# Expert weights fetched as 2 KB and 8 KB runs, two blocks to a transfer, with the rows of the expert inputs permuted to match

## The chip, the cores and the metric

The kernel runs on one core of a Trainium2 chip. The metric is device time in microseconds (us); lower is better. All inputs and outputs lie in device memory (HBM) in float32. The engines are called PE (TensorE, matrix products), DVE (VectorE), ACT (ScalarE), POOL (GpSimd) and SP (SyncE, which here only issues transfers).

## The reference

One decoder layer over 512 tokens of width 1024. First a layer norm with modulation from a condition vector, three kinds of attention, an output projection, a residual and a layer norm. Then, on the result `x`, the part that the change is about:

```
h   = LN(x) * (1 + scale2) + shift2
y   = MoE(h)                       # 16 experts in 4 groups; each token: one group, two experts in it
x   = LayerNorm(alpha * x + (1 + gate2) * y)

MoE:  g = h @ w_gate[e]   u = h @ w_up[e]        # [1024 -> 256] each, 16 experts
      a = silu(g) * u * combine[e]
      y = sum over e of a @ w_down[e]            # [256 -> 1024]
```

The weights of the 16 experts are 16 x (2 x 1024 x 256 + 256 x 1024) x 4 bytes = 50.3 MB, the largest input.

## The kernel before, in words

Everything is one function `build`. A scheduler orders the instructions of each engine from the program and a table of numbers `PRM`; the queues are in order, so an instruction that waits holds back all behind it on its engine. SP issues nearly all loads.

Attention and the output projection come first. `outproj(n)` (line 1184) works on 128 tokens: product, layer norm to `x1`, and at line 1238 ACT writes the normalised row block `t2`, which POOL stores to the scratch tensors `xsA_d` (tokens 0 to 255) or `xs_d` in HBM (line 1240). `route(n)` (line 1059) then picks the experts: long chains of small DVE steps, with the products `rkp` (line 1097), `tabp` (1129) and `tabq` (1163) on PE, ending in a table of token numbers (`tokA` at line 1135 after block 1, `tokB` at 1131 after block 3). While PE waits there it runs dummy products called `warm` (line 350).

The expert stage goes over four quarters q of four experts each. `prep(q)` (line 1297) gathers token rows from `xsA_d` and `xs_d` by those tables (POOL, line 1289, three row tiles b of 128 slots), transposes them 128 channels at a time (`gTp`, line 997) and lets ACT apply scale and shift while it copies them to `gT` (line 1002). The scale and the shift of channel block k are columns of `mc2` and `mc1`, one channel to a partition, made by `mod_cols` (line 335). In block k, partition p holds channel 128 k + p.

Per quarter PE then does (lines 1313 to 1321) for each of eight channel blocks k and three row tiles b one set of four products, one per expert, which run side by side on 32 columns each. `gu` collects gate and up together, 512 wide. After silu, product and transposes (`atp`, line 1346; `aT`), lines 1360 to 1372 do the down projection `dn` in two column halves hf of 512, for three b and two blocks f of 128 hidden channels, again four experts side by side. `cmb` and `cmh` (lines 1410, 1418) add up the results per token, DVE and ACT do the last layer norm, and POOL scatters rows to the output (line 1394).

The weights come through a ring of eight buffers of 8 KB per partition (`ewt`, line 1281; six in pool `wst`, two in `wst2`, `PRM["NW"]`). For gate and up, a buffer holds one block k of four experts and is filled by two transfers of 512 KB, in runs of 1 KB (line 1316). For down, a buffer holds one f and one hf of four experts, one transfer of 1 MB in runs of 2 KB (line 1365); so a quarter takes 8 + 4 buffers, and the two down buffers of hf=0 are given back halfway through the down projection. A buffer is refilled when its last product is done.

Of the kernel before, what the change touches and what calls it, by code (L numbers as in the profile page):

```python
# [10 lines left out]
F32 = mybir.dt.float32  # L11
F32R = mybir.dt.float32r
I32 = mybir.dt.int32
AF = mybir.ActivationFunctionType
OP = mybir.AluOpType
# [28 lines left out]
T, D, NT, KD = 512, 1024, 4, 8  # L44
# [64 lines left out]
def build(tc, A, out, dbg=None):  # L109
# [30 lines left out]
    with top:  # L140
# [7 lines left out]
        def wt(name, p):  # L148
            return p.tile([128, 2048], F32, name=name, tag="w")
# [10 lines left out]
        gt_d = dram.tile([4, 512], F32, name="gt_d")  # L160

# [515 lines left out]
        gate_out(0, m1)  # L677
        zc = {"k": kp.tile([128, 16, 32], F32, name="zck"), "v": kp.tile([128, 16, 32], F32, name="zcv")}
# [334 lines left out]
        sc2 = lambda k: mc2[:, k // 4, k % 4:k % 4 + 1]  # L1013
        sh2 = lambda k: mc1[:, 2 + k // 4, k % 4:k % 4 + 1]
# [169 lines left out]
        def outproj(n):  # L1184
# [53 lines left out]
            S.activation(t2, x1, AF.Identity, bias=nm, scale=rs2)  # L1238
# [42 lines left out]
        def ewt(name):  # L1281
            i = cnt_w[0]
            cnt_w[0] += 1
            return wt(name, wst if i % (NW1 + NW2) < NW1 else wst2).rearrange("p (e c) -> p e c", e=4)
# [25 lines left out]
        for q in range(NQ):  # L1310
            gT = gTn
            gu = [psp.tile([128, 512], F32, name=f"gu{b}", tag=("q", "z", "z")[b], bufs=(1, 2, 2)[b]) for b in range(CAPB)]
            for k in range(KD):
                w = ewt(f"gu{q}_{k}")
                for u, nm in enumerate(("moe_w_gate", "moe_w_up")):
                    SP.dma_start(w[:, :, 256 * u:256 * u + 256],
                                 A[nm][4 * q:4 * q + 4, k * 128:(k + 1) * 128].rearrange("e p f -> p e f"))
                for b in range(CAPB):
                    together([lambda e=e: PE.matmul(gu[b][32 * e:32 * e + 32], gT[b][:, k, 32 * e:32 * e + 32], w[:, e],  # L1319
                                                    start=(k == 0), stop=(k == KD - 1), skip_group_check=True)  # L1320
                              for e in range(4)])
# [18 lines left out]
            for b in range(CAPB):  # L1340
                a = ep.tile([128, 256], F32, name="act", bufs=2)
                S.activation(a, gu[b][:, 0:256], AF.Silu)  # L1342
                V.tensor_tensor(a, a, gu[b][:, 256:512], op=OP.mult)  # L1343
                ps = bank("t", "atp2")
                for f in range(2):
                    PE.transpose(ps[:, f * 128:(f + 1) * 128], a[:, f * 128:(f + 1) * 128], ident)
                t = ep.tile([128, 2, 128], F32, name="aT", bufs=4)
                cp(pick("aTe", "V", b), t, heads(ps[:, 0:256], 2))
                aT.append(t)
                s = q * CAPB + b  # L1350
                o = ep.tile([128, GW], F32R, name="oht", bufs=CAPB)
                V.tensor_scalar(o[:, 0:min(GW, 256)], C("pos", 0, min(GW, 256)), tab[:, 2 * NSLOT + s:2 * NSLOT + s + 1], None, op0=OP.is_equal)
                if GP > 128:
                    G.tensor_copy(o[:, 256:320], o[:, 128:192])
                oht.append(o)
# [4 lines left out]
            for hf in range(2):  # L1360
                cs = slice(512 * hf, 512 * hf + 512)
                dn = [psp.tile([128, 512], F32, name=f"dn{b}", tag=("s", "s", "o")[b], bufs=(2, 2, 1)[b]) for b in range(CAPB)]
                wd = [ewt(f"dn{q}_{hf}{f}") for f in range(2)]
                for f in range(2):
                    SP.dma_start(wd[f], A["moe_w_down"][4 * q:4 * q + 4, f * 128:(f + 1) * 128, cs].rearrange("e p c -> p e c"))
                k_ = "3" if q == NQ - 1 else ""

                for b in range(CAPB):
                    for f in range(2):
                        together([lambda b=b, e=e, f=f: PE.matmul(  # L1370
                            dn[b][32 * e:32 * e + 32], aT[b][:, f, 32 * e:32 * e + 32], wd[f][:, e],
# [99 lines left out]
        with tc.If(cnt > CAP), tc.tile_pool(name="bp", bufs=1) as bp:  # L1471
# [19 lines left out]
            with tc.For_i(0, NE, 1) as e:  # L1491
                wg = bp.tile([128, KD, 512], F32, name="bwg")
                wd = bp.tile([128, 2, D], F32, name="bwd")
                for u, nm in enumerate(("moe_w_gate", "moe_w_up")):
                    SP.dma_start(wg[:, :, 256 * u:256 * u + 256],
                                 A[nm][ds(e, 1)].rearrange("a (k p) f -> p (a k) f", p=128))
# [74 lines left out]
```

## Time and profile before

| | us |
|---|---|
| three runs | 591.91, 593.4, 599.62 (median 593.4) |
| the profiled execution | 596.7 |
| its span | 594.8 |
| PE busy in it | 548.7 (92%) |
| DVE busy | 368.2 (62%) |
| ACT busy | 222.1 (37%) |
| POOL busy | 97.4 (16%) |
| mean share of the 16 DMA engines used by SP's loads | 52.9% |
| bytes read from HBM | 112.12 MB |

The span is divided into 40 slices in the page's rows; one slice is 14.9 us. Busy shares are means over stages that have different limits, so what a change is worth has to be read in the stage where it lies. The expert stage is roughly the last third, from 402 us on. A number behind "PEclk" is the clock granted to PE, 1.00 being the higher of its two levels.

### The profile page before, as it was taken

To read this page: it belongs to the slowest core of one execution; us is meant where nothing else is said; L and a number is where in the kernel's file an instruction comes from. 1 tells how busy PE (TensorE), PEld (TensorE's weight loads), DVE (VectorE), ACT (ScalarE), POOL (GpSimd) and SP (SyncE) were. 2 spreads that over 40 slices of the span, in tenths; PEclk is the share of its full clock that TensorE was granted. 3 is DMA by queue.
4 is the path that set the end of the run, shared out by engine and by line. 5 is a ranking of instruction groups with operands and counts; after the bars stand their busy time and mean duration, and the time that the engine had idled before them with its cause. 6 is when DMAs were issued, how large, how long until landed. Compare 5 with 4: busy or idle time off the path is not lost.

```text
span 594.8 us, 10444 instructions
## 1 busy us (share of the span) xinstructions
PE 548.7 (92%) x3856; PEld 333.1 (56%) x3856; DVE 368.2 (62%) x1219; ACT 222.1 (37%) x556; POOL 97.4 (16%) x114
## 2 busy tenths in 40 slices
PE   2899999999899999999899999978899999999990
PEld 1559775687788998755455456653434234234240
DVE  7515656664678568877769568886138157167174
ACT  2514443561428336374634512121434062070130
POOL 0114200000010010003301112123502122011022
PEclk9969999999799999999999999978999999999996
DMA  8993246743930200098300685359699999999601
GB/s 301 373 328 108 83 142 225 260 153 102 323 91 19 72 37 1 2 220 226 124 2 0 222 278 200 119 209 306 164 370 351 366 365 348 374 356 354 248 1 47
DMA packets 77546, 117.05 MB, mean 197 GB/s; under 512 B 7937, under 2 KB 54440, under 8 KB 77492
## 3 DMA queue, kind: packets, MB, share of 16 engines
q1 hardware_dynamic: 72328, 102.60, 52.9%
q0 software_dynamic: 4960, 13.64, 6.3%
q8 instruction: 32, 0.52, 0.4%
q14 instruction: 22, 0.18, 0.1%
q10 hardware_dynamic: 204, 0.11, 0.1%
HBM read 112.12 MB, written 8.40 MB: 203 GB/s over the span
## 4 chain that ended last, share of the span: by engine, by line
PE 78%; DVE 11%; issue 3%; DMA 3%; ACT 2%; POOL 2%; ACTq 0%; POOLq 0%
PE gu L1319 13%; PE zps L407 13%; PE dn L1370 7%; PE onsa L894 6%; PE yps L1215 5%; PE zall L423 3%; PE modps L323 2%; PE modps L375 2%; PE gTp L997 2%; PE cmb L1410 2%; PE stp L501 2%; PE sps L921 2%; PE wps L849 1%; PE warm L356 1%; PE cmh L1418 1%
## 5 line engine op out<-in xcount | busy, mean ns | idle before, releaser
L1319 PE MATMUL gu<-gu,gT 128*32 128x512 f32 x768 | 85.3, 596 | 0.1
L1319 PEld LDWEIGHTS gu<-gu,gT 128*32 128x32 f32 x768 | 23.8, 110 | 52.5 <-issue 50.6
L1370 PE MATMUL dn<-dn,aT 128*32 128x512 f32 x384 | 45.3, 597 | 0.4 <-ACT aT L127 0.2
L1343 DVE TENSOR_TENSOR act<-act,gu 128x256 f32<-128x256 f32 x12 | 5.1, 421 | 59.8 <-ACT act L1342 59.8
L1002 ACT ACTIVATE gT<-gTp,modc,modc 128x128 f32<-128x128 f32 x96 | 35.7, 461 | 10.1 <-PE gTp L997 9.5
L1342 ACT ACTIVATE act<-gu 128x256 f32<-128x256 f32 x12 | 4.6, 387 | 72.1 <-PE gu L1319 72.1
L1215 PE MATMUL yps<-wol,oM 128*128 128x512 f32 x64 | 30.9, 595 | 0.0
L1375 DVE SCALAR_TENSOR_TENSOR y<-dn,tab,gt 128x512 f32<-128x512 f32 x24 | 18.0, 748 | 10.2 <-PE dn L1370 10.2
L323 PE MATMUL modps<-ada,cond 128*32 128x512 f32 x128 | 18.3, 631 | 4.4 <-DVE gr L1079 4.1
L1370 PEld LDWEIGHTS dn<-dn,aT 128*32 128x32 f32 x384 | 10.4, 109 | 20.8 <-issue 18.5
L894 PE MATMUL onsa<-pt,vs 128*64 128x512 f32 x40 | 20.6, 614 | 0.0
L491 ACT ACTIVATE Sg<-Sg,nms 128x128 f32<-128x128 f32 (+3 forms) x32 | 17.8, 559 | 3.7 <-DVE nms L490 3.3
L491 ACT ACTIVATE W<-W,nmw 128x256 f32<-128x256 f32 (+1 forms) x32 | 15.3, 478 | 9.7 <-DVE nmw L490 9.3
L997 PEld LDWEIGHTS gTp<-cf,rows 128*128 128x128 f32 x96 | 10.4, 142 | 15.1 <-ACT gT L1002 9.2
L448 DVE TENSOR_TENSOR rp<-zps,trig 128x128 f32<-128x128 f32 (+1 forms) x28 | 9.7, 345 | 12.9 <-PE zps L407 12.5
L356 PE MATMUL warm<-cf 128*128 128x128 f32 x88 | 17.2, 326 | 0.1
L407 PE MATMUL zps<-B1s,hH 128*128 128x256 f32 x64 | 15.1, 329 | 2.2 <-DVE B1s L210 1.1
L356 PEld LDWEIGHTS warm<-cf 128*128 128x128 f32 x88 | 13.8, 222 | 5.5 <-issue 4.7
L1378 DVE TENSOR_TENSOR ys<-y,ys 128x512 fp32r<-128x512 f32 x22 | 15.2, 692 | 2.1 <-ACT ys L127 1.4
L997 PE MATMUL gTp<-cf,rows 128*128 128x128 f32 x96 | 14.8, 282 | 1.6 <-DMA rows<-xs_d,tokB 1.6
L127 ACT COPY pt<-stp 128x512 f32<-128x512 f32 x14 | 7.9, 586 | 22.2 <-PE stp L501 21.9
L1389 ACT ACTIVATE R<-R,rsf 128x1024 f32<-128x1024 f32 x3 | 3.7, 1241 | 31.4 <-DVE rsf L1388 31.4
(529 smaller groups left out, 1472.7 us busy)
## 6 DMA issues: line engine op xcount, KB each, us to landing
ada<-in_ada_w_dram SPq DMA_DIRECT2D x48, 512.0 KB, 5.9
gu<-in_moe_w_gate_dram SPq DMA_DIRECT2D x32, 512.0 KB, 9.7
gu<-in_moe_w_up_dram SPq DMA_DIRECT2D x32, 512.0 KB, 9.6
dn<-in_moe_w_down_dram SPq DMA_DIRECT2D x16, 1024.0 KB, 10.5
x<-in_x_dram SPq DMA_DIRECT2D x4, 512.0 KB, 4.9
phik<-in_nsa_phi_k_dram SPq DMA_DIRECT2D x4, 512.0 KB, 5.0
phiv<-in_nsa_phi_v_dram SPq DMA_DIRECT2D x4, 512.0 KB, 4.8
wo<-in_w_out_dram SPq DMA_DIRECT2D x8, 256.0 KB, 9.3
```

The lines of the kernel that those rows point to most:

```text
L323: return lambda: PE.matmul(ps[32 * j:32 * j + 32], cond[:, k], t[:, 512 * (j % 2):512 * (j % 2) + 512], start=first, stop=last, skip_group ...
L356: PE.matmul(ps[:, :128], ident, ident, start=True, stop=True)
L407: PE.matmul(ps[:, :w], l[:, k, ts_], get(k, r), start=(k == 0 and i == 0), stop=(k == KD - 1 and i == 2))
L423: m = PE.matmul(outs[n], l[:, k, n * 128:(n + 1) * 128], get(k, r), start=(beg and n % 2 == 0), stop=(k == KD - 1 and i == 2), skip_group_ ...
L491: S.activation(S_h, S_h, AF.Exp, bias=nm, scale=-1.0, accum_out=den)
L894: PE.matmul(ops[64 * g:64 * g + 64, cols], lhsT, rhs, start=first[g], stop=False, skip_group_check=True)
L997: PE.transpose(ps[:, k * 128:(k + 1) * 128], src[:, (4 * a + k) * 128:(4 * a + k + 1) * 128], ident)
L1002: S.activation(dst[:, kk], pk, AF.Identity, bias=sh2(kk), scale=sc2(kk))
L1215: last = PE.matmul(ps, l, r[:, cs], start=(i == 0), stop=(i == len(order) - 1))
L1319: together([lambda e=e: PE.matmul(gu[b][32 * e:32 * e + 32], gT[b][:, k, 32 * e:32 * e + 32], w[:, e], start=(k == 0), stop=(k == KD - 1), ...
L1370: together([lambda b=b, e=e, f=f: PE.matmul(dn[b][32 * e:32 * e + 32], aT[b][:, f, 32 * e:32 * e + 32], wd[f][:, e], start=(f == 0), stop= ...
L1375: V.scalar_tensor_tensor(y, dn[b], tab[:, s:s + 1], gt2[:, cs], op0=OP.mult, op1=OP.mult)
```

## The change

The gate and up weights of two neighbouring blocks come in one buffer. Partition p now holds channels 8 p to 8 p + 7 instead of p, 128 + p, 256 + p and so on, so that two blocks k, k + 1 lie next to each other in HBM: runs of 2 KB at a pitch of 8 KB, four experts, 1 MB per transfer. The down weights of two experts come in one buffer with hidden channels 2 p and 2 p + 1 on partition p: runs of 8 KB, 2 MB per transfer, both halves hf and both f in it. The ring has four buffers of 16 KB instead of eight of 8 KB. To match, `t2` is written with its channels permuted, the transposes of the activations read every second column, and scale and shift of the gathered rows come from a new tile `mpk`, which is made by a trip through HBM (`md_d`: two small stores, two small loads).

```diff
-    "NW": [6, 2, 3, 5], ...
+    "NW": [3, 1, 3, 5], ...
         def wt(name, p):
-            return p.tile([128, 2048], F32, name=name, tag="w")
+            return p.tile([128, 4096], F32, name=name, tag="w")
+        md_d = dram.tile([4, 512], F32, name="md_d")
         gate_out(0, m1)
+        SP.dma_start(md_d[0:2], m1[64:128:32])
...
-        sc2 = lambda k: mc2[:, k // 4, k % 4:k % 4 + 1]
-        sh2 = lambda k: mc1[:, 2 + k // 4, k % 4:k % 4 + 1]
+        SP.dma_start(md_d[2:4], m2[0:64:32])
+        mpk = cst.tile([128, 2, KD], F32, name="mpk")
+        for a in range(2):
+            SP.dma_start(mpk[:, a], md_d[2 * a:2 * a + 2].rearrange("a (p k) -> (a p) k", k=KD))
+        V.tensor_scalar(mpk[:, 1], mpk[:, 1], 1.0, None, op0=OP.add)
+        sc2 = lambda k: mpk[:, 1, k:k + 1]
+        sh2 = lambda k: mpk[:, 0, k:k + 1]
...
-            S.activation(t2, x1, AF.Identity, bias=nm, scale=rs2)
+            S.activation(t2.rearrange("t (k p) -> t p k", k=KD), x1.rearrange("t (p k) -> t p k", k=KD), AF.Identity,
+                             bias=nm, scale=rs2)
...
             for k in range(KD):
-                w = ewt(f"gu{q}_{k}")
-                for u, nm in enumerate(("moe_w_gate", "moe_w_up")):
-                    SP.dma_start(w[:, :, 256 * u:256 * u + 256],
-                                 A[nm][4 * q:4 * q + 4, k * 128:(k + 1) * 128].rearrange("e p f -> p e f"))
+                if k % 2 == 0:
+                    wg = ewt(f"gu{q}_{k}").rearrange("p (e u k f) -> p e u k f", e=4, u=2, k=2)
+                    for u, nm in enumerate(("moe_w_gate", "moe_w_up")):
+                        SP.dma_start(wg[:, :, u], A[nm][4 * q:4 * q + 4].rearrange("e (p k) f -> p e k f", k=KD)[:, :, k:k + 2])
                 for b in range(CAPB):
-                    ... gT[b][:, k, 32 * e:32 * e + 32], w[:, e],
+                    ... gT[b][:, k, 32 * e:32 * e + 32], wg[:, e, :, k % 2],
...
-                    PE.transpose(ps[:, f * 128:(f + 1) * 128], a[:, f * 128:(f + 1) * 128], ident)
+                    PE.transpose(ps[:, f * 128:(f + 1) * 128], a[:, f:256:2], ident)
...
-                wd = [ewt(f"dn{q}_{hf}{f}") for f in range(2)]
-                for f in range(2):
-                    SP.dma_start(wd[f], A["moe_w_down"][4 * q:4 * q + 4, f * 128:(f + 1) * 128, cs].rearrange("e p c -> p e c"))
+                if hf == 0:
+                    wd = [ewt(f"dn{q}_{a}").rearrange("p (e f c) -> p e f c", e=2, f=2) for a in range(2)]
+                    for a in range(2):
+                        SP.dma_start(wd[a], A["moe_w_down"][4 * q + 2 * a:4 * q + 2 * a + 2].rearrange("e (p f) c -> p e f c", f=2))
...
-                            ... aT[b][:, f, 32 * e:32 * e + 32], wd[f][:, e],
+                            ... aT[b][:, f, 32 * e:32 * e + 32], wd[e // 2][:, e % 2, f, cs],
```

The branch for overfull experts behind the stage is changed in the same way; it is not entered with these inputs.

The change also moves instructions. Three places follow; lines of the changed file are a few higher than before (`rkp` 1104 and 1105, `tabp` 1137, `gu` 1328, `warm` 357, `dn` 1380, `gTp` 999, `atp` 1355).

PE while the last token block is routed. `gu_0`, `gu_1`, ... are weight buffers, named by their first block k; `rkp` and `tabp` are products of `route(3)`. Before:

```order
L1096 MATMUL rkp<-base,cf 128x20
L1096 MATMUL rkp<-asg_3530,ones 128x20
L1097 MATMUL rkp<-asg_3531,cf 128x20
L1319 MATMUL gu_4794<-gu_3_4842,gT 32x512 x4
L356 MATMUL warm<-cf 128x128 x5
L1319 MATMUL gu_4794<-gu_4_4857,gT 32x512 x4
L356 MATMUL warm<-cf 128x128
L1319 MATMUL gu_4794<-gu_5_4872,gT 32x512 x4
L1319 MATMUL gu_4794<-gu_6_4887,gT 32x512 x4
L1129 MATMUL tabp<-rh,ohp 128x12 x2
```

The same stretch with the change:

```order
L1104 MATMUL rkp<-base,cf 128x20
L1328 MATMUL gu_4801<-gu_2_4831,gT 32x512 x4
L1104 MATMUL rkp<-asg_3537,ones 128x20
L1105 MATMUL rkp<-asg_3538,cf 128x20
L357 MATMUL warm<-cf 128x128
L1328 MATMUL gu_4801<-gu_4_4858,gT 32x512 x4
L357 MATMUL warm<-cf 128x128 x3
L1328 MATMUL gu_4801<-gu_4_4858,gT 32x512 x4
L357 MATMUL warm<-cf 128x128 x2
L1137 MATMUL tabp<-rh,ohp 128x12 x2
```

Between the last `rkp` and `tabp` stood four sets of `gu` and six `warm`; now two sets and six `warm` stand there. One set moved ahead of the last two `rkp`; the others moved behind `tabp`, the last of them behind the first transposes of the gathered rows.

PE where the down projection of quarter 0 begins; `aT` are the activations, `dn_0` and `dn_1` the new down buffers (experts 0, 1 and experts 2, 3 of the quarter). Before:

```order
L1370 MATMUL dn_4976<-dn_00_4979,aT 32x512 x4
L1370 MATMUL dn_4976<-dn_01_4980,aT 32x512 x4
L1346 MATMUL atp_4956<-cf,act 128x128
L997 MATMUL gTp<-cf,rows_4662 128x128 x4
L1346 MATMUL atp_4956<-cf,act 128x128
L1370 MATMUL dn_4977<-dn_00_4979,aT 32x512 x4
```

With the change:

```order
L1380 MATMUL dn_4971<-dn_0_4974,aT 32x512 x2
L1380 MATMUL dn_4972<-dn_0_4974,aT 32x512 x2
L1355 MATMUL atp_4951<-cf,act 128x128
L999 MATMUL gTp<-cf,rows_4669 128x128 x4
L1355 MATMUL atp_4951<-cf,act 128x128
L1380 MATMUL dn_4971<-dn_1_4975,aT 32x512
L1380 MATMUL dn_4972<-dn_1_4975,aT 32x512
L1380 MATMUL dn_4971<-dn_1_4975,aT 32x512
L1380 MATMUL dn_4972<-dn_1_4975,aT 32x512
```

The first two sets of four products are split into halves there; in the later quarters each set stands together as before.

POOL near the end of `outproj(2)`; `yrs` is the reciprocal deviation of a layer norm, `rows` a gathered row tile. Before:

```order
L1234 DMA x_d<-yt 128x1024
L1208 TENSOR_TENSOR yrs_4285<-ymv_4284,half 128x1
L1289 DMA rows_4662<-xsA_d,tokA 128x1024
L1240 DMA xs_d<-t_4232 128x1024
L1208 TENSOR_TENSOR yrs_4439<-ymv_4438,half 128x1
```

With the change:

```order
L1242 DMA x_d<-yt 128x1024
L1298 DMA rows_4669<-xsA_d,tokA 128x1024
L1216 TENSOR_TENSOR yrs_4292<-ymv_4291,half 128x1
L1249 DMA xs_d<-t_4239 128x1024
L1216 TENSOR_TENSOR yrs_4446<-ymv_4445,half 128x1
```

The first gather now stands ahead of the second `yrs` of block 2.

## Rows read from the trace of the kernel before

**Rows 1.** Part 2 of the page: busy tenths in 40 slices of the span, and what the DMA engines moved.

```profile
PE   2899999999899999999899999978899999999990
DMA  8993246743930200098300685359699999999601
GB/s 301 373 328 108 83 142 225 260 153 102 323 91 19 72 37 1 2 220 226 124 2 0 222 278 200 119 209 306 164 370 351 366 365 348 374 356 354 248 1 47
```

**Rows 2.** The chain of work that ended last, in order of time, in quarters 1 and 2 of the expert stage: start us, length us, what.

```profile
459.22 20.74 PE gu L1319 x192
...
495.79 2.99 PE cmb L1410 x12
498.78 2.05 PE cmh L1418 x8
500.83 20.74 PE gu L1319 x192
...
522.62 1.07 PE dn L1370 x8
```

**Rows 3.** Busy time in stretches: from:to, length, then busy us of PE, PEld, DVE, ACT and POOL with counts, granted clock, DMA share, GB/s.

```profile
459.20:480.00 20.80, 20.80 (x194) 6.20 (x194) 5.35 (x12) 2.01 (x3) 3.70 (x6) 1.00 1.06 370
480.00:500.80 20.80, 20.75 (x152) 9.42 (x154) 16.34 (x33) 10.91 (x29) 5.52 (x7) 1.00 1.05 353
...
470.00:480.00 10.00, 10.00 (x97) 2.88 (x90) 0.84 (x2) 0.77 (x2) 0.00 (x0) 1.00 1.05 394
...
504.00:512.00 8.00, 8.00 (x80) 2.40 (x76) 2.45 (x2) 0.96 (x1) 1.07 (x1) 1.00 1.05 351
```

**Rows 4.** SP's queue in order of time: start us, length us until the last of the group was issued, line, what.

```profile
122.97 0.37 SPq L695 DMA_DIRECT2D phik<-in_nsa_phi_k_dram  x1
138.25 0.51 SPq L345 DMA_DIRECT2D gt_d<-mod  x1
...
267.29 0.38 SPq L1018 DMA_DIRECT2D rwm<-in_router_w_dram  x1
...
278.13 14.59 SPq L192 DMA_DIRECT2D ada<-in_ada_w_dram  x4
...
428.44 3.80 SPq L1365 DMA_DIRECT2D dn<-in_moe_w_down_dram  x4
...
464.25 8.60 SPq L1365 DMA_DIRECT2D dn<-in_moe_w_down_dram  x4
```

**Rows 5.** Part 6 of the page: transfers by line, how many, size of one, median us from issue to landing.

```profile
phik<-in_nsa_phi_k_dram SPq DMA_DIRECT2D x4, 512.0 KB, 5.0
...
yt<-in_x_dram SPq DMA_DIRECT2D x4, 512.0 KB, 3.2
```

**Rows 6.** PE in order of time while block 3 is routed: start us, length us, line, what, idle before it and its cause.

```profile
408.76 0.40 PE L1097 MATMUL rkp<-asg,cf 128*128 128x20 f32 x2 [2.73 <-DVE asg L1088]
409.09 1.17 PE L1319 MATMUL gu<-gu,gT 128*32 128x512 f32 x8
410.18 2.50 PE L356 MATMUL warm<-cf 128*128 128x128 f32 x10
...
416.21 0.61 PE L1129 MATMUL tabp<-rh,ohp 128*128 128x12 f32 x4
```

**Rows 7.** DVE in order of time in the same stretch.

```profile
411.57 0.23 DVE L1126 TENSOR_SCALAR rh<-oht,cf 128x24 f32<-128x24 f32 x1
...
416.87 0.17 DVE L1131 TENSOR_TENSOR tokB<-tab,tabp 128x12 int32<-128x12 f32 x1 [4.45 <-PE tabp L1129]
```

**Rows 8.** PE's busy time, granted clock, DMA share and GB/s in stretches of 1 us.

```profile
406.00:407.00 1.00, 0.03 (x1) 1.00 1.02 364
...
410.00:411.00 1.00, 1.00 (x8) 0.50 1.09 383
...
421.00:422.00 1.00, 0.00 (x0) 1.00 0.66 226
```

**Rows 9.** The chain that ended last, at the start of the expert stage.

```profile
417.79 4.25 DMA rows<-xs_d,tokB
...
423.30 1.92 PE gu L1319 x16
...
427.39 11.30 PE gu L1319 x104
438.68 0.38 PE atp L1346 x2
...
439.09 0.38 ACT aT L127
...
439.51 1.92 PE dn L1370 x16
```

**Rows 10.** POOL in order of time around the first gather.

```profile
376.29 0.57 POOL L1208 TENSOR_TENSOR yrs<-ymv,half 128x1 f32<-128x1 f32 x1 [1.00 <-DVE sc L1106]
380.71 1.12 POOL L1289 DMA_INDIRECT rows<-xsA_d,tokA  x1 [3.85 <-DVE tokA L1135]
```

**Rows 11.** DVE in order of time: the last sum into the modulation row `m1`, and the place of the new step on `mpk`, in a wait of DVE.

```profile
112.00 0.69 DVE L537 TENSOR_TENSOR mod<-modps,mod 128x512 f32<-128x512 f32 x1
...
295.75 0.18 DVE L923 RECIPROCAL dns<-dns 128x4 f32<-128x4 f32 x1 [1.77 <-ACT Sg L491]
```

**Rows 12.** ACT in order of time: the last of the four writes of `t2`.

```profile
394.02 1.24 ACT L1238 ACTIVATE t<-yt,ynm,yrs 128x1024 f32<-128x1024 f32 x1 [10.19 <-DVE key L1099]
```

**Rows 13.** Groups by line from 400 us on: the transposes of the activations, count, busy us, mean ns of one.

```profile
L1346 PE MATMUL atp<-cf,act 128*128 128x128 f32 x24 | 5.4, 296 | 0.0
```

More of the change, by code (lines that the diff above doesn't have):

```diff
@@ L1283, in ewt @@
             cnt_w[0] += 1
-            return wt(name, wst if i % (NW1 + NW2) < NW1 else wst2).rearrange("p (e c) -> p e c", e=4)
+            return wt(name, wst if i % (NW1 + NW2) < NW1 else wst2)
         x1g_ = [wraw(f"x1g{i}") for i in range(4)]
@@ L1313, in build @@
             for k in range(KD):
-                w = ewt(f"gu{q}_{k}")
-                for u, nm in enumerate(("moe_w_gate", "moe_w_up")):
-                    SP.dma_start(w[:, :, 256 * u:256 * u + 256],
-                                 A[nm][4 * q:4 * q + 4, k * 128:(k + 1) * 128].rearrange("e p f -> p e f"))
+                if k % 2 == 0:
+                    wg = ewt(f"gu{q}_{k}").rearrange("p (e u k f) -> p e u k f", e=4, u=2, k=2)
+                    for u, nm in enumerate(("moe_w_gate", "moe_w_up")):
+                        SP.dma_start(wg[:, :, u], A[nm][4 * q:4 * q + 4].rearrange("e (p k) f -> p e k f", k=KD)[:, :, k:k + 2])
                 for b in range(CAPB):
-                    together([lambda e=e: PE.matmul(gu[b][32 * e:32 * e + 32], gT[b][:, k, 32 * e:32 * e + 32], w[:, e],
+                    together([lambda e=e: PE.matmul(gu[b][32 * e:32 * e + 32], gT[b][:, k, 32 * e:32 * e + 32], wg[:, e, :, k % 2],
                                                     start=(k == 0), stop=(k == KD - 1), skip_group_check=True)
@@ L1370, in build @@
                         together([lambda b=b, e=e, f=f: PE.matmul(
-                            dn[b][32 * e:32 * e + 32], aT[b][:, f, 32 * e:32 * e + 32], wd[f][:, e],
+                            dn[b][32 * e:32 * e + 32], aT[b][:, f, 32 * e:32 * e + 32], wd[e // 2][:, e % 2, f, cs],
                             start=(f == 0), stop=(f == 1), skip_group_check=True) for e in range(4)])
@@ L1495, in build @@
                     SP.dma_start(wg[:, :, 256 * u:256 * u + 256],
-                                 A[nm][ds(e, 1)].rearrange("a (k p) f -> p (a k) f", p=128))
+                                 A[nm][ds(e, 1)].rearrange("a (p k) f -> p (a k) f", p=128))
                 SP.dma_start(wd, A["moe_w_down"][ds(e, 1)].rearrange("a (k p) c -> p (a k) c", p=128))
```

2 rows, old and new, of the table PRM are left out of this document.

## Prediction

> **What bounds the kernel now.** I first read the page's slices [rows 1]: in the last third PE is full, and so are the DMA engines, at 348 to 374 GB/s. Two resources that are both full don't say which sets the pace, so I next read the chain of waits in order of time [rows 2]. There the reader is to see that PE's pieces follow on each other: gate and up begin at 459.22 and again at 500.83, 41.61 us later, and the piece before each is PE's own. No transfer stands in the chain of quarters 1 to 3. PE sets the pace there and the weights arrive just in time. What the DMA engines gain in those quarters is worth nothing as such; it matters only if it keeps the weights on time.
>
> Time that is not PE work lies ahead of it, where block 3 is routed. PE waits 2.73 us for the assignment, DVE then 4.45 us for the product `tabp`, and the gather for the token table takes 4.25 us to land [rows 6, 7, 9]. A change of order there counts at once.
>
> **What shorter and longer runs are worth to the DMA engines.** The stretches [rows 3] show it in this kernel. Around 504 to 512 us gate and up weights in 1 KB runs are moving: 351 GB/s. At 470 to 480 us it is the down weights, issued from 464.25 us on [rows 4], in 2 KB runs: 394 GB/s. So I take 394 GB/s for all weights after the change (12% more), with 350 as the low end, if a run of 2 KB in every 8 KB is no better than 1 KB runs, and 410 as the high end for 8 KB runs. Per quarter the engines now move 20.8 x 0.370 + 20.8 x 0.353 = 15.0 MB [rows 3], of which 12.6 MB are weights (50.3 MB / 4) and 2.4 MB gathers and scatters.
>
> The Trainium skill ("DMA: Bandwidth & Descriptors", section "Where 436 GB/s comes from") says that for transfers between HBM and SBUF the HBM side binds at about 358 GB/s. By that, longer runs would gain nothing, and the sum would be that of the first rival below. The 394 GB/s [rows 3] are above it, so I give the rule little weight.
>
> **The coarser ring, quarters 1 to 3.** The ring keeps its 64 KB per partition, but the grain doubles, and the two down buffers now serve both halves, so both are given back only at the end of the down projection, where two of four were given back halfway. In order, a quarter's buffers are four of gate and up, then two of down. With four slots, the third and fourth gate and up buffers of the next quarter wait for the two down buffers of this one. Behind them on SP's in-order queue stand the next two down transfers. So between the end of one down projection (495.79) and the start of the next (522.62), 26.83 us [rows 2], four buffers of 2.097 MB must come, 8.39 MB, besides about half of the gathers, 1.2 MB. That is 9.6 MB / 0.394 = 24.4 us. Starting and landing a transfer cost extra: 512 KB take 5.0 us in one place and 3.2 us in another [rows 5], less 1.3 us for the bytes at 394 GB/s leaves 1.9 to 3.7 us; I take 2.8. Together 27.2 us against 26.8: the fourth arrives 0.4 us late, in each of three quarters. **Plus 1.2 us**; from 0 (410 GB/s and 1.9 us) to 10 (350 GB/s).
>
> **Quarter 0, down projection.** In the order with the change `dn_0` is asked for when buffer `gu_0` is free, three sets of `gu` before `dn_1`, and 11 sets before the end of gate and up. A set takes 11.30 / 13 = 0.87 us [rows 9], so 9.6 us, then `atp` and `aT` with 0.8 us, then the two half sets on `dn_0` and some transposes, 2.5 us: 12.9 us until the first product on `dn_1`. The load takes 4.19 / 0.394 = 10.6, plus 2.8, plus 0.7 for gathers in between: 14.1. PE waits 1.2 us (0 to 3.7). Before, the transfers for the first half alone, 2.1 MB, had to be there, issued from 428.44 for 439.51 [rows 4, 9]. The split sets cost as well: four products run side by side in the time of one, so two half sets take 1.7 us, and the four single ones behind them about 2.2, for what took 1.7 (two sets). Plus 2.2. **Together plus 3.4 us** (2 to 6).
>
> **Routing of block 3.** `rh` is ready at 411.8 (411.57 + 0.23), yet `tabp` comes at 416.21, because from 409.1 PE works off four sets of `gu` and the `warm` products in its order [rows 6, 7]. With the change two sets and the same `warm` stand there. They took longer than needed: PE's clock was at half from 410 on, after an idle stretch in which PE did almost nothing at 406 to 407 [rows 8]. One moved set now fills 0.9 of those 2.73 us, and 1.8 us are left; the idle stretch around 421 us did not lower the clock [rows 8]. So I expect full clock: two sets 1.8 us, twelve `warm` passes at half of 2.50 / 10 = 0.25 us plus a little, 2.0, so `tabp` at about 413 instead of 416.2. **Minus 3.1 us** (minus 1.5 if the clock still falls). Against it, one set that filled the wait for the gather now stands behind the first transposes: **plus 0.9 us**.
>
> **POOL's order.** The gather of 1.12 us, which waits for `tokA`, now stands ahead of a `yrs` that used to be done at 376.9 [rows 10]. DVE's order puts its part of that layer norm later too, so the `yrs` comes at about 382.4, and the steps of block 3 start somewhat later. **Plus 0.6 us** (0 to 1.1).
>
> **What is hidden.** `m1` is complete at 112.7 [rows 11], before its store's place on SP's queue behind 112 us; the first `mpk` load stands between the issues at 122.97 and 138.25, where SP waits anyway [rows 4]. The second store stands ahead of 267.29; its load holds the queue until it has landed, a few us, and the four `ada` loads behind it were not issued before 278.13 [rows 4]. If that cover were gone they would start some us later, with over 100 us until their products. The DVE step on `mpk` stands in a wait of 1.77 us [rows 11]. All zero; at worst 1 us.
>
> The permuted write of `t2` I take at its old price, 1.24 us [rows 12], four times, mostly in gaps of ACT; the trace has no ACT write of this form, so from 0 to plus 3.7 us each (four times the time), of which at most two lie on the path. The transposes that read every second column stay at 296 ns [rows 13]; doubled, 24 of them would cost 7 us, a third of it on the path. `gu` reads two pieces of 256 instead of 512 together; I take zero.
>
> The Trainium skill ("SBUF — State Buffer", section "Door 1: The DMA port swizzle (why `[64,N]` ≈ `[32,N]`)") says that SBUF works in lines of 16 bytes and that each access to a new line costs extra, so float32 is free up to a stride of 4. By that the transposes (stride 2) cost nothing and the `t2` writes (stride 128) do; no row here shows a strided write, and the third rival is what it would give.
>
> **The sum.** 1.2 + 3.4 - 3.1 + 0.9 + 0.6 = plus 3.0 us. On the profiled execution, 596.7 with a span of 594.8 (1.9 us lie around it), that is 599.7. The profiled execution lies 3.3 us above the median of the runs, 593.4, so on their scale the forecast is **596.4 us**, plus 0.5%. A measurement of this kernel can tell about 2% (11.9 us) from no change.
>
> **Rivals.**
> First, slower: the coarse ring starves PE. In its favour: the ring's last slots are asked for late in every quarter, and 26.8 us for 9.6 MB leave no reserve. It decides below some 390 GB/s. At 350 GB/s each quarter is late by 9.6 / 0.350 + 2.8 - 26.8 = 3.4 us, three times 10.3, and quarter 0 waits 1.3 us longer: 9.1 + 1.3 over the forecast, 607 us. Against it: 394 GB/s with 2 KB runs today. At 370 GB/s it is 5 us over, 601.
> Second, the ring is hidden: at 410 GB/s and 1.9 us of start no transfer is late and only the split sets cost: 3.0 - 1.2 - 1.2 = plus 0.6, 594 us.
> Third, strided writes and reads cost: two `t2` writes at 3.7 us, 604 us. Against it: ACT was idle for 10.19 us before the last write [rows 12], so there is slack.
> Fourth, faster: the shorter routing counts in full, the split sets run beside each other better than I think and no transfer is late: minus 3, 590 us. A faster run by 12 us would need work on PE to go, and none does.
>
> **How the numbers follow.** Forecast 0.42, first rival 0.2 (half of it over 2%), second 0.2, third 0.08, fourth 0.1. From 590 to 606 us holds eight in ten: below it lies part of the fourth, above it the worst of the first and third. Slower by over 2% (above 605.3): half of the first and a little of the third, 0.12. Faster by over 2%: 0.02. Within 2%: 0.86.
>
> **What would show it.** In the profile after: DMA share below 1 and a dip in the second half of each down projection; GB/s near 394 in gate and up stretches; PE idle before `dn` with a down transfer as the cause, near 1 us in quarter 0 and below 1 us later; `tabp` 3 us earlier behind `rkp` and no half clock there; the quarter's period near 42.0 us. A period of 44 or more would make the first rival right; a period of 41.6 the second.

## The result and the profile after

The changed kernel took 598.11 us (median of 20 runs) beside 594.6 us for the kernel before (20 runs): ratio 1.0055, 95% interval 1.0031 to 1.0079, so 0.3 to 0.8% slower. The forecast was 596.4 on a scale on which the kernel before stood at 593.4, that is +0.5%, with 590 to 606 as its range. The time is that of the likeliest case, but its terms did not all come out: in the expert stage the run is nearer to the second rival (the ring hidden, the split sets at a cost), and terms that were put at nothing made up the rest, as the sections below show.

First the expert stage, in the chain that ended last (start us, length us, what):

```profile
439.55 1.91 PE dn L1380 x8
...
442.21 0.12 PE atp L1355
442.33 2.71 PE dn L1380 x16
...
456.10 2.98 PE cmb L1420 x12
459.08 2.07 PE cmh L1428 x8
461.15 20.74 PE gu L1328 x192
...
482.99 1.25 PE dn L1380 x8
...
498.02 2.99 PE cmb L1420 x12
501.01 2.05 PE cmh L1428 x8
503.06 20.74 PE gu L1328 x192
...
524.90 1.07 PE dn L1380 x8
```

As before [rows 2], PE's pieces follow on each other. The period is 41.91 us, then 41.72 (544.78 for the next `gu`), against 41.61. The first eight passes of `dn` show when the second down buffer came: 1.07 us where nothing waits, 1.25 in quarter 1. So the coarse ring made PE wait 0.2 us once (in the second trace of the changed kernel, same_again, in quarters 1 and 2: 1.24 and 1.25 us). What the engines did is in the stretches (from:to, length, busy us of PE, PEld, DVE, ACT, POOL, granted clock, DMA share, GB/s):

```profile
461.10:472.00 10.90, 10.90 (x105) 3.39 (x108) 4.54 (x10) 1.24 (x1) 3.72 (x6) 1.00 1.05 398
472.00:482.00 10.00, 10.00 (x97) 2.91 (x87) 0.84 (x2) 0.77 (x2) 0.00 (x0) 1.00 1.01 417
...
493.50:498.00 4.50, 4.50 (x42) 1.25 (x41) 3.21 (x6) 1.62 (x5) 0.98 (x1) 1.00 0.45 160
498.00:503.00 5.00, 5.00 (x26) 3.56 (x22) 4.93 (x10) 0.00 (x0) 0.62 (x2) 1.00 0.76 259
```

398 GB/s in a stretch that moves mostly the 2 KB runs (the down transfers are issued from 466.50 us on), 417 in the stretch of the 8 KB runs; before it was 351 and 394 [rows 3]. And the foreseen dip: at the end of the down projection the engines are busy 45% of the time, since both down buffers are still held. PE is busy throughout, as before. The transfers got faster, and nothing had waited for them.

Now the routing of block 3, PE in order of time (start, length, line, what, idle before and its cause):

```profile
409.98 0.40 PE L1105 MATMUL rkp<-asg,cf 128*128 128x20 f32 x2 [1.63 <-DVE asg L1096]
410.22 0.47 PE L357 MATMUL warm<-cf 128*128 128x128 f32 x2
410.62 1.93 PE L1328 MATMUL gu<-gu,gT 128*32 128x512 f32 x8
412.48 1.64 PE L357 MATMUL warm<-cf 128*128 128x128 f32 x6
414.05 1.07 PE L1328 MATMUL gu<-gu,gT 128*32 128x512 f32 x8
415.05 0.71 PE L357 MATMUL warm<-cf 128*128 128x128 f32 x4
415.60 0.51 PE L1137 MATMUL tabp<-rh,ohp 128*128 128x12 f32 x4
```

PE's clock in stretches of 1 us there, which still fell to the lower level:

```profile
410.00:411.00 1.00, 1.00 (x8) 0.79 0.98 375
411.00:412.00 1.00, 1.00 (x8) 0.50 1.07 416
```

And DVE in the same place:

```profile
411.05 0.19 DVE L1151 TENSOR_TENSOR sc<-ohs,aff 128x32 f32<-128x32 f32 x1
...
413.99 0.23 DVE L1134 TENSOR_SCALAR rh<-oht,cf 128x24 f32<-128x24 f32 x1
...
416.15 0.17 DVE L1139 TENSOR_TENSOR tokB<-tab,tabp 128x12 int32<-128x12 f32 x1 [1.69 <-PE tabp L1137]
```

DVE's wait for `tabp` fell from 4.45 [rows 7] to 1.69 us, but `rh` itself came later: DVE's order now works off the affinities (`aff`, lines 1151 to 1154, four steps) ahead of the first step on the ranks (line 1119), and `rh` lies 4.01 us behind the start of `rkp` where it was 2.81 before [rows 6, 7].

ACT's four writes of `t2` took 2.16 to 2.27 us each, against 1.24 [rows 12] (two of them):

```profile
338.30 2.16 ACT L1246 ACTIVATE t<-yt,ynm,yrs 128x1024 f32<-128x1024 f32 x1
...
395.79 2.18 ACT L1246 ACTIVATE t<-yt,ynm,yrs 128x1024 f32<-128x1024 f32 x1 [10.28 <-DVE key L1107]
```

A place that the prediction passed over is the `ada` load ahead of block 3. Before, PE and SP:

```profile
390.63 1.94 PE L323 MATMUL modps<-ada,cond 128*32 128x512 f32 x8 [4.07 <-DVE gr L1079]
```

```profile
385.33 2.19 SPq L192 DMA_DIRECT2D ada<-in_ada_w_dram  x4
```

and after:

```profile
392.36 1.94 PE L324 MATMUL modps<-ada,cond 128*32 128x512 f32 x8 [4.82 <-DMA ada<-in_ada_w_dram]
```

```profile
387.02 2.08 SPq L193 DMA_DIRECT2D ada<-in_ada_w_dram  x4
```

The load is issued 1.7 us later, and PE's product with it. The first row is put down to DVE; its length (5.3 us behind the issue, as after) says that it was the load.

Last the transposes of the activations, groups by line from 400 us on: 324 ns against 296 [rows 13].

```profile
L1355 PE MATMUL atp<-cf,act 128*128 128x128 f32 x24 | 5.9, 324 | 0.0
```

### Where the time went, stage by stage

Each stage runs from the start of one product on PE to that of the next, in us. Each kernel has two traces here (the second ones are from the experiments).

| stage | before | before, again | after | after, again |
|---|---|---|---|---|
| span's start to first `oswa` | 184.89 | 181.07 | 185.55 | 182.14 |
| to `lsum` of block 0 | 164.01 | 163.96 | 164.44 | 164.45 |
| to `lsum` of block 3 | 52.79 | 52.29 | 52.92 | 53.81 |
| to `tabp` of block 3 | 14.52 | 16.05 | 12.69 | 12.69 |
| to first `dn` of quarter 0 | 23.30 | 23.37 | 23.95 | 25.63 |
| to first `cmb` | 14.72 | 14.71 | 16.48 | 16.47 |
| to first `cmb` of quarter 3 | 120.94 | 120.95 | 121.59 | 121.81 |
| to the span's end | 19.63 | 19.10 | 19.18 | 19.70 |

The first stage swings by 4 us for either kernel. From `oswa` on it is 409.9 and 410.4 us before, 411.3 and 414.6 after: 2.7 us more in the mean, of the same size as the 3.5 us between the medians.

### The profile page after: what moved, and what is told of

It reads as the page before. It is cut to its first block, busy times and chain, and to the rows that moved or that the text cites. A ratio compares the mean times of both kernels' runs of the same rounds, so it can differ in the third digit from the quotient of the medians.

```text
span 596.8 us, 10373 instructions
## 1 busy us (share of the span) xinstructions
PE 551.3 (92%) x3856; PEld 333.9 (56%) x3856; DVE 369.3 (62%) x1220; ACT 224.8 (38%) x556; POOL 98.0 (16%) x114
## 4 chain that ended last, share of the span: by engine, by line
PE 74%; DVE 10%; DMA 7%; issue 3%; ACT 3%; POOL 2%; ACTq 0%; POOLq 0%; SPq 0%
PE gu L1328 13%; PE zps L408 13%; PE dn L1380 8%; PE onsa L896 5%; PE yps L1223 5%; DMA ada<-in_ada_w_dram 3%; PE modps L324 3%; PE gTp L999 2%; PE cmb L1420 2%; PE zall L424 2%; PE sps L923 2%; PE stp L502 2%; DMA A1r<-in_w_in_dram 2%; PE wps L851 1%; PE cmh L1428 1%
## 5 line engine op out<-in xcount | busy, mean ns | idle before, releaser
L1380 PE MATMUL dn<-dn,aT 128*32 128x512 f32 x384 | 47.2, 597 | 0.3 <-ACT aT L127 0.2
L1004 ACT ACTIVATE gT<-gTp,mpk 128x128 f32<-128x128 f32 x96 | 35.5, 462 | 26.3 <-PE gTp L999 25.7
L424 PE MATMUL zall<-A2s,hH 128*128 128x184 f32 x64 | 14.7, 330 | 1.5 <-ACT hH L394 1.5
```

The source lines that it names most:

```text
L424: m = PE.matmul(outs[n], l[:, k, n * 128:(n + 1) * 128], get(k, r), start=(beg and n % 2 == 0), stop=(k == KD - 1 and i == 2), skip_group_ ...
L1004: S.activation(dst[:, kk], pk, AF.Identity, bias=sh2(kk), scale=sc2(kk))
L1380: together([lambda b=b, e=e, f=f: PE.matmul(dn[b][32 * e:32 * e + 32], aT[b][:, f, 32 * e:32 * e + 32], wd[e // 2][:, e % 2, f, cs], start ...
```

## The experiments

### The changed kernel again

> The changed kernel once more, unaltered. The times gave +0.55% (3.3 us) over the kernel before. Question: is the 1.2 us by which the routing of block 3 starts later (its first sum `lg` at 403.24 against 402.03 us) one of order or of chance. Theory A, order (one more microsecond of output projection stands on PE ahead of the modulation product, and the `ada` loads behind it are issued at 387.0 instead of 385.3): `lg` lies again near 403 and the distance from `tabp` of block 2 to the `modps` behind the load is again near 13 us (before: 11.3). Theory B, chance: that distance is back near 11.3. Time +0.3 to +0.8% in both.

Measured: 598.23 us, ratio 1.0069 (1.0034 to 1.0104). `lsum` to `tabp` of block 3 again 12.69 us, and from the `tabp` ahead of it to the waiting `modps` 13.53 us (the expectations call that `tabp` block 2's; counted from 0, as in the table above, it is block 1's). Theory A for both places.

### The kernel before again

> The kernel before once more, unaltered, for its trace alone. The changed kernel's traces have 12.69 us from `lsum` to `tabp` of block 3 and 13.1 to 13.9 us from `tabp` of block 2 to the `modps` that waits for its `ada` load. Theory A, both are of the order: here 14.5 and 11.5 us again, to 0.3 us. Rival B, chance: either lies within 0.3 us of the changed kernel's. Where the first products of the stage (`oswa`) lie, 179 to 186 us so far, follows the half clock in the first 60 us and around 150 us in both theories.

Measured in its one profiled execution (593.3 us): 11.73 us up to `modps`, as foreseen, and this time the row names the load:

```profile
387.00 1.82 PE L323 MATMUL modps<-ada,cond 128*32 128x512 f32 x8 [4.33 <-DMA ada<-in_ada_w_dram]
```

`lsum` to `tabp` of block 3 took 16.05, not 14.5: the same four sets, more of them at the lower clock. So the routing gain of the new order is 1.8 us or more (12.69 against 14.52 and 16.05), and part of it depends on the clock.

### Down buffers by column half

```diff
-                if hf == 0:
-                    wd = [ewt(f"dn{q}_{a}")... for a in range(2)]       # two experts each, both halves
+                wd = ewt(f"dn{q}_{hf}").rearrange("p (e f c) -> p e f c", e=4, f=2)   # four experts, one half
```

> Down buffers by column half (four experts, 512 columns, 2 KB runs, given back halfway) in place of by pair of experts; the orders on PE and DVE up to the first down product are the same. Theory A: the whole growth of the down projection of quarter 0 (16.55 against 14.79 us from first `dn` to `cmb`) is split sets, two half sets and four single products that take 3.7 us where two sets take 1.85. Then it is back at 14.8, the time is 1.8 us below the changed kernel, and the dip of the DMA engines at the end of each down projection is gone, which is worth nothing more. Rival B: part of it is a wait for the second down load; the first half needs the same 2 MB by then, so the stretch stays above 15.5. Rival C: the early return of buffers counts: periods of quarters 1 to 3 fall below 41.6 us and the time by 2.5 us or more.

Measured: 596.31 us, ratio 1.004 (1.0004 to 1.0075), 1.9 us below the changed kernel measured beside it (same_again), with overlapping intervals; the trace decides. The chain in quarter 0:

```profile
434.11 1.92 PE dn L1380 x16
...
448.95 2.98 PE cmb L1420 x12
```

14.84 us, all of the growth gone, with 388 GB/s at the end of a down projection (485.0 to 490.5 us) in place of 160. Theory A in the trace; B falls. Period 41.73, not below 41.61: C falls, the early return is worth nothing. Half a set takes as long as a whole one: the two half sets of the changed kernel 1.91 us, two whole sets here 1.92.

### Run length alone

```diff
-  SP.dma_start(wg[:, :, u], ...rearrange("e (p k) f -> p e k f", k=KD)[:, :, k:k + 2])
+  SP.dma_start(wg[:, :, u]..., ...rearrange("e (j p k) f -> p (e j) k f", j=2, k=4)[:, :, k // 2])
```

> Gate and up weights in 1 KB runs again, in the same buffers, transfers and order (4 experts x 2 pieces of 1 KB per partition; rows of a transfer then are others than the activations' channels; gate and up lie 8 KB apart in the buffer). Theory A (the first rival's price): the engines fall from 395 to 410 to about 350 GB/s in gate and up stretches, the coarse ring has less than 2 us of slack, and quarters 1 to 3 become late by 1.5 to 3.4 us each: 4 to 10 us more than the changed kernel, with PE idle before `gu` or `dn` for a weight load. Rival B: the coarse ring has 3.4 us of slack or more; the rate falls but no product waits: the same time as the changed kernel within 1 us. Rival C: the rate does not follow the run length: 390 GB/s or more and the same time.

Measured: 598.86 us, ratio 1.007 (1.0034 to 1.0107), 0.6 us above the changed kernel, not to be told apart. The first 10 us of gate and up in quarter 1, after and with 1 KB runs:

```profile
461.10:471.10 10.00, 10.00 (x97) 1.00 1.06 397
```

```profile
464.40:474.40 10.00, 10.00 (x97) 1.00 1.10 360
```

The rate falls, and the second down buffer is then late; the first eight passes of `dn` take

```profile
486.35 2.25 PE L1380 MATMUL dn<-dn,aT 128*32 128x512 f32 x8
```

2.25 us in place of 1.07: 1.2 us in quarter 1, 0.9 in quarter 2. By the time this is rival B, by the trace theory A: the mechanism of the first rival is there, at a third of its price of 3.4 us a quarter. So the long runs do have a use, 1 us a quarter in this trace, but only against a wait that the coarse ring brings with it.

### `t2` in its old order

```diff
-            S.activation(t2.rearrange("t (k p) -> t p k", k=KD), x1.rearrange("t (p k) -> t p k", k=KD), AF.Identity,
+            S.activation(t2, x1, AF.Identity,
```

> `t2` written in its old order (the gathered channels then don't match the weights' rows; all instructions stand in the same order on every engine). The strided write took 2.20 us against 1.245, four times. Theory A: about one of the four 0.95 us lies on the path (the copy of `x1T` waits 0.8 us for ACT): 1 us less than the changed kernel, `lg` of block 3 earlier by 0.5 to 1. Rival B: all lie beside other work: no change within 0.3 us in the distances between products of blocks 2 and 3. Rival C: two or more count: 2 us or more less.

Measured: 596.28 us, ratio 1.0042 (1.0012 to 1.0071). In the trace `oswa` to `lsum` of block 0 is 164.04 us, as before; with the strided write 164.44. From there to `lsum` of block 3 52.78 against 52.92. So 0.4 us at block 0 and next to nothing at blocks 1 to 3, where the later `ada` load covers it. Between B and A. The medians of this run and of same_again beside it differ by 2 us, more than the trace has, but their intervals overlap.

### Earlier steps of the second gate: before, twice, and the changed kernel

```diff
-    "ORD": "... s2 s1 s2 o1 o2 s2 o3 L"
+    "ORD": "... s2 s1 s2 o1 g1 o2 s2 g1 o3 L"
```

> The kernel before with both steps of the second gate's modulation product put behind blocks 1 and 2 of the output projection in the program's list of stages, so that their `ada` loads no longer stand behind each other at 385 us. PE idled 4.07 us there, and the transposes of block 3 behind it could have begun when `yt` was there (389.62 + 0.74 = 390.36) and not at 392.57. Theory A: 2.2 us less than the kernel before, no PE wait for `ada` after 300 us. Rival B: DVE is the next bound there (it is 90% busy) and the 1.9 us of products moved ahead of it lengthen the block before: no change within 1 us.

> The kernel before with the earlier steps of the second gate, once more, beside the next two on the same chip. The first time it took 589.25 us against 595.01 (ratio 0.986), and the changed kernel with down buffers by half and the same steps 592.93. Theory: 0.983 to 0.990 again.

> The changed kernel with down buffers by column half and with the same earlier steps of the second gate. Theory A: the changed kernel lost time in two places, split sets of quarter 0 (1.9 us, gone with buffers by half) and the later `ada` load (about 1.7 us and more); with both gone it is within 1 us of the kernel before with the same earlier steps, and 4 to 5 us below the changed kernel, about 593.5 us. If the gain of the routing order (1.8 us) stays, 592. Rival B: something else of the change costs 2 us or more, then it stays above 595.5.

Measured: 589.25 us, ratio 0.986 (0.981 to 0.991), then, on another chip, 591.41 us, ratio 0.9974 (0.9934 to 1.0015): the intervals don't meet, the second measurement doesn't bear out the size of the first, and the theory for it failed. From `oswa` to the end both traces have 406.3 and 407.8 us, 2 to 4 below the kernel before. The wait for the load is gone, and what PE waits for there is DVE, as rival B had it:

```profile
390.15 1.97 PE L1231 MATMUL x1p<-cf,yt 128*128 128x128 f32 x8 [4.59 <-DVE yt L1228]
```

But the gain does not lie there. From `oswa` to `lsum` of block 3 both traces have 218.5 us, 1.7 to 2.3 more than the kernel before (216.8 and 216.3); the gain is in the stage behind it, `lsum` to `tabp` of block 3, with 9.2 us in both against 14.5 and 16.1. Neither theory had that. Before, DVE and POOL (its last fill, `MEMSET`) show in that stage:

```profile
402.63 4.08 DVE L1142 TENSOR_SCALAR aff<-th 128x16 f32<-128x16 f32 x1
```

```profile
406.14 0.54 POOL L1328 MEMSET x1g<- 128x512 f32 x1
```

and with the earlier steps DVE shows:

```profile
401.35 0.17 DVE L1142 TENSOR_SCALAR aff<-th 128x16 f32<-128x16 f32 x1
```

In every trace with the stages in their old order, the changed kernel's too, six fills of POOL run from 0.4 to 5.0 us behind the start of `lsum`, and four small steps of DVE beside them take 3.8 to 4.1 us each and end when the last fill ends. With the earlier steps the fills stand ahead of `lsum`, and the same steps take 0.16 to 0.17 us. That the fills hold DVE is read from these times; no run moved the fills alone.

The changed kernel with down buffers by half and these steps took 592.93 us, ratio 0.9957 (0.9922 to 0.9991): as theory A had it by the time (593.5), but not within 1 us of the kernel before with the same steps: 1.5 to 3.7 us above it. So something else costs, if less than rival B said. In the traces it is 1.6 us, from `oswa` to `lsum` of block 3 (220.1 against 218.5). At block 2 DVE shows what:

```profile
386.64 0.17 DVE L1077 SCALAR_TENSOR_TENSOR bia<-th,rb 128x16 f32<-128x16 f32 x1 [0.89 <-ACT th L1076]
```

and ACT ahead of it:

```profile
384.36 2.23 ACT L1246 ACTIVATE t<-yt,ynm,yrs 128x1024 f32<-128x1024 f32 x1 [6.97 <-DVE ynm L1245]
386.41 0.20 ACT L1076 ACTIVATE th<-lg 128x16 f32<-128x16 f32 x1
```

The step `th` of the routing stands behind the strided `t2` on ACT, and DVE, which is now the bound, waits 0.89 us for it.

### The strided write without the cover

> The changed kernel with down buffers by half and the earlier steps, and `t2` written in its old order (the gathered channels then don't match the weights' rows; the order is the same on every engine). With the strided write, DVE waited 0.89 us for `th`, which stands behind `t2` of block 2 on ACT, and the gathered rows' copies stood 0.9 us later behind `t2` of block 3; with `lsum` of block 2 to `tabp` of block 2's table 15.88 us against 14.21 in the kernel before with the same steps. Theory A: without the `ada` wait the strided write is on the path twice, and 0.4 us once more at block 0: 2 us less than with it, about 591 us, and the 15.88 us fall to 14.2. Rival B: it is PE's half clock there (8 `warm` at 2.06 us against 1.73) that makes the difference: above 15 us still, no change in time beyond 0.5.

Measured: 590.61 us, ratio 0.9952 (0.9916 to 0.9989). The median is 2.3 us below that of half_and_early, but on another chip, and the two ratios (0.9952 and 0.9957) don't differ; the times decide nothing. In the trace `oswa` to `lsum` of block 3 is 218.5 us, as in the kernel before with the same steps. `lsum` of block 2 to `tabp` fell from 15.88 to 14.57 us, with PE's clock at half during the `warm` products in both (8 `warm` 2.05 and 2.06 us). Of these 1.3 us, 0.9 lie ahead of `x1p`, where DVE's wait is gone; the other 0.4 lie behind it, where the clock came back sooner (six `gTp` in 0.90 us, not 1.49), which is rival B's part:

```profile
382.08 0.18 DVE L1077 SCALAR_TENSOR_TENSOR bia<-th,rb 128x16 f32<-128x16 f32 x1
```

Theory A in the place, with 1.6 us; the total of this one execution is only 0.5 us shorter (407.3 against 407.8 from `oswa` on), because its clock fell again behind `tabp` (two sets `gu` in 3.45 us).

> As half_and_early, but only neighbouring pairs of channels lie on a partition, and ACT reads every second column and writes `t2` contiguous, so the transposes read contiguous columns again. Transfers in 2 KB runs as before it. The Trainium skill ("SBUF — State Buffer", section "Door 1: The DMA port swizzle (why `[64,N]` ≈ `[32,N]`)") has float32 free up to a stride of 4. Theory A: a step of two elements costs ACT nothing, the four rows of `t2` are back at 1.25 us, the time is that of `t2` in its old order within 0.7 us, about 591. Rival B: any step that isn't 1 costs ACT: about 2.2 us each, the time stays at 593.

```diff
+  S.activation(t2.rearrange("t (k j p) -> t k j p", k=4, j=2), x1.rearrange("t (k p j) -> t k j p", k=4, j=2), ...
```

Measured: 591.04 us, ratio 0.9944 (0.9903 to 0.9985). ACT's write:

```profile
382.95 1.33 ACT L1246 ACTIVATE t<-yt,ynm,yrs 128x1024 f32<-128x1024 f32 x1 [6.97 <-DVE ynm L1245]
```

1.33 us, and 1.32 to 1.33 in all four: a step of two elements costs 7%, not nothing and not 77%. Theory A for ACT and, within the interval, for the time; but half_and_early's ratio is no different, so the time does not show the use of it. Nor does this trace: `oswa` to `lsum` of block 3 is 219.8 us, against 218.5 in half_early_t2 and 220.1 in half_and_early. At block 1 DVE waited longer than in half_early_t2 (0.30 us) for a store to land:

```profile
363.39 0.69 DVE L1225 TENSOR_TENSOR t<-yps,gt 128x512 f32<-128x512 f32 x1 [1.11 <-DMA x_d<-yt]
```

and at block 2 PE's clock stayed low for longer (the set `gu` ahead of `tabp` took 1.68 us, not 1.07). With the earlier steps before_early, half_and_early and this kernel are all below both kernels by their medians (the second measurement of before_early is not clear of the kernel before), and no difference between the layouts is left that these runs can tell.

### Pairs, read by the transposes

```diff
-  PE.transpose(..., src[:, (4 * a + k) * 128:(4 * a + k + 1) * 128], ident)
+  PE.transpose(..., src[:, (4 * a + k) // 2 * 256 + k % 2:(4 * a + k) // 2 * 256 + 256:2], ident)
```

> Only neighbouring pairs of channels on a partition (256 kk + 2 p + j) in place of eight: `t2` is written in its old order, the transposes of the gathered rows read every second column instead, the same transfers in 2 KB runs with the pair as one contiguous stretch. The transposes of the activations show what reading every second column costs: weight load 208 against 142 ns, product 284 against 273. Theory A: 96 transposes `gTp` at 11 ns more, 1 us less or nothing on the path, `t2` at 1.25 us again beside other work: the same time as the changed kernel within 1 us. Rival B: the weight load of 66 ns more is not hidden: 64 transposes on PE's path in quarters 0 to 3 cost 4 us more. Rival C: the contiguous stretch per expert makes the transfers faster; worth nothing on the time.

Measured: 599.06 us, ratio 1.0054 (1.0018 to 1.0091), as the changed kernel: theory A. All instructions of the line (min, median, max ns):

```profile
L999 PEld LDWEIGHTS gTp<-cf,rows x96: 193/209/261, 395.0 to 534.8; 128*128 128x128 f32 x96
L999 PE MATMUL gTp<-cf,rows x96: 277/284/487, 395.0 to 534.9; 128*128 128x128 f32 x96
```

209 and 284 ns against 140 and 273 in the changed kernel. The period is 42.2 us against 41.7 to 41.9, so some 0.3 to 0.5 us a quarter of it show. By the Trainium skill ("SBUF — State Buffer", section "Door 1: The DMA port swizzle (why `[64,N]` ≈ `[32,N]`)") a stride of two would be free; for PE's weight load it isn't, and most of the price (24 weight loads a quarter at 69 ns more) lies under the products.

### Transfers split in two

```diff
+  for u, nm, j in [(u, nm, j) for j in (0, 2) for u, nm in enumerate(("moe_w_gate", "moe_w_up"))]:
+      SP.dma_start(wg[:, j:j + 2, u], A[nm][4 * q + j:4 * q + j + 2]...)
```

> The changed kernel with each gate and up transfer split in two of 512 KB (two experts each, still 2 KB runs, same buffers). As many gate and up transfers as in the kernel before then stand in the program, and the orders go back to those of before where the output projection ends: five `yps` and not nine between `lsum` and the `modps` of block 2, `yrs` ahead of the first gather on POOL; while block 3 is routed, five sets of `gu` and a part of a sixth stand ahead of the second `tabp`, and split sets still open the down projection. Theory A: the changed kernel's later `ada` load and its shorter routing are effects of this order: `tabp` of block 2's first `lsum` to `modps` behind the load is back near 11.5 us, `lsum` to `tabp` of block 3 back at 14.5 to 17 us, and the time is 1 to 4 us above the changed kernel. Rival B: the distances stay at 13.2 and 12.7, the order has no part in them, same time.

Measured: 599.52 us, ratio 1.0104 (1.0048 to 1.016). From `tabp` of block 1 (block 2 in the expectation) to `modps` it is 11.93 us, `lsum` to the second `tabp` of block 3 14.70:

```profile
385.53 1.20 PE L324 MATMUL modps<-ada,cond 128*32 128x512 f32 x8 [4.53 <-DMA ada<-in_ada_w_dram]
```

Theory A for the order: the later load and the shorter routing both come and go with the number of gate and up transfers that the scheduler places. The time doesn't bear on it: 0.35% above the changed kernel by the two ratios is inside the intervals, and 2.3 us more of this trace lie in quarters 1 to 3 (123.9 us from `cmb` to `cmb`, not 121.6). Unexpected: with 393 GB/s in gate and up, `dn` of quarter 1 again waits 1 us (first eight passes 2.12 us) and that of quarter 2 1.4 us, where the second half sets name the transfer:

```profile
521.19 1.05 PE L1380 MATMUL dn<-dn,aT 128*32 128x512 f32 x4 [0.37 <-DMA dn<-in_moe_w_down_dram]
```

So the ring's reserve depends on the size of a transfer as well as on the rate; why was not tried.

## Why the prediction was right, and where it was not

**PE sets the pace, the engines' gain is worth nothing.** Right: 398 and 417 GB/s, and the same 20.74 us of `gu`.

**Coarse ring, plus 1.2 us.** Mis-sized: 0.2 us, in one quarter or two. The rate was 398 to 417 and not 394, and 0.4 us a quarter was that near to nothing (at 400 GB/s the prediction's own sum gives 24.0 + 2.8 = 26.8 us, in time). The rate alone does not set it: split_transfers had 393 GB/s and waited 1.0 and 1.4 us. The dip was as described.

**Quarter 0, plus 3.4 us.** Its part of 2.2 for the split sets was the whole: 1.8 measured. The wait of 1.2 for the second buffer did not occur: in the chain above `dn` goes on at 442.33, right behind `atp`. That the split sets are the cause is shown by down_by_half.

**Routing, minus 3.1 us.** The direction was right, and the size 1.8 against one trace of before, 3.4 against the other. Two assumptions failed in detail: the clock did fall to half (0.50 at 411), and DVE's order, which the prediction did not look at there, put `rh` 1.2 us later. It also took PE's wait for the assignment as given; DVE is late there beside POOL's fills (4.08 us for a step of 0.17), in both kernels alike.

**Gate and up set behind the transposes, plus 0.9.** 0.65 us (23.95 against 23.30), and 2.3 us where the clock fell there.

**POOL's order, plus 0.6.** `yrs` came at 382.39, as said (382.4). What delays block 3, though, is the `ada` load, 1.7 us later. It stands behind four more products of the output projection on PE, the same new order (0.9 us of the 1.7; the rest stays open). This mechanism was missing from the prediction. PE's and POOL's part were not separated: both went back together in split_transfers.

**`t2` at its old price.** Wrong: 2.2 us, inside the bounds given (up to 3.7 more). On the path of the changed kernel it costs 0.4 us, at block 0, with the others covered by the `ada` load; with the earlier steps, without that cover, 1.6 us in all, 0.9 of it at block 2.

**Strided transposes, zero.** The stage from `cmb` to `cmb` of quarter 3 is 0.35 us longer in down_by_half, where ring and split sets are out of play.

**What is hidden, zero.** With `t2` in its old order the stage up to `lsum` of block 0 is 164.04 us against 164.01 before, so the second store, its load and the step on `mpk` cost nothing there. The first ones lie in the first stage, whose swing of 4 us would hide a small cost. `gu` takes 20.74 us with two pieces as with one.

So the sum by the traces is 0.2 + 1.8 - 1.8 + 0.65 + 0.4 + 0.35, with 0.1 to 1.5 for the later load (the stage up to `lsum` of block 3; all traces with the new order and without the earlier steps have 52.8 to 54.6 us there, those with the old one and split_transfers 52.3 to 52.8): 1.7 to 3.1 us, against plus 3.0 forecast and 1.8 to 4.7 timed (0.31 to 0.79% of 594.6). That the total was met so closely is partly luck: ring and buffer wait were set 2.6 us too high, the routing gain 1.3 too high, the load and the writes too low.

## What to carry to other kernels

Faster transfers pay only where a product waits for one; look for that row before changing a layout. A coarser buffer has its own prices, above all sets of products torn apart where the first of two buffers arrives alone. And where a scheduler sets the order, halving the number of transfers moves instructions far from them: read the new order of every engine, DVE's and the other loads' too, at each place with a wait. Last, a wait that is gone is not yet a gain: the earlier steps removed a wait of 4 us for a load and won nothing there, and their gain lay in a stage where POOL's fills no longer stood beside DVE's steps. Compare stage by stage before naming a cause.

## What the runs showed of the hardware

Much of the spread between executions lies in the first 185 us: `oswa` starts between 178.9 and 186.2 us in the fourteen traces. From there on two traces of one kernel differ by 0.5 us (before), 1.5 (before_early) and 3.3 (the changed kernel). PE's granted clock in the first stage differs from one execution to the next. Over the first 178 us it is 0.98 where `oswa` comes at 179.1 to 179.3, and 0.92 to 0.93 where it comes at 185.5 to 186.2. At 30 to 40 us it is 0.50 in the trace of before (`oswa` at 184.89 us) and 0.84 in that of down_by_half (179.30), where the two kernels do the same work.

```profile
30.00:40.00 10.00, 10.00 (x60) 0.50 1.08 356
```

```profile
30.00:40.00 10.00, 9.79 (x81) 0.84 1.06 350
```

Four float32 products of 32 columns each, issued one behind the other, take 0.96 us together (two such sets 1.92 us), and two of them alone take the same (two half sets 1.91 us). An ACT write with a step of 128 elements took 2.2 us for 128x1024, a read with a step of two 1.33, a contiguous copy 1.24. Four DVE steps of 0.17 us lasted about 4 us while POOL's fills ran beside them.
